# The first block's down-projection by seven products, and the differences of w_down made earlier, one operation at a time

## The chip, the cores and the metric

The kernel runs on one core of a Trainium2 chip. A core has a matrix engine (TensorE, PE in the profile, with its weight loads as PEld), a vector engine (VectorE, DVE), a scalar engine (ScalarE, ACT), a general engine (GpSimd, POOL) and an engine that here only issues transfers (SyncE, SP). Each takes its own instructions in order; transfers (DMA) run on 16 engines of their own and are issued from the queues of SP, ACT and POOL. The metric is the time of one execution on the device, in microseconds (us).

## The reference: what is computed

One layer of an encoder is computed for 2048 prompt rows and for 8 x 16 = 128 sample rows: 17 tiles of 128 rows, of width 1024. The first half is attention and a recurrent memory, whose results are joined and multiplied by `w_out`. The second half, which the change touches, is a feed-forward network with a convolution of width 3 over the rows:

```python
    mix = jnp.concatenate([att, mlstm_out], axis=-1) @ w_out
    x = x + rms_norm(mix, norm_g[1])
    ffn, new_buf = conv_ffn(rms_norm(x, norm_g[2]), conv_buf, w_up, w_conv, b_conv, w_down)
    x = x + rms_norm(ffn, norm_g[3])

def conv_ffn(h, buf, w_up, w_conv, b_conv, w_down):
    u = h @ w_up                                   # 1024 -> 2 * 2816
    ext = jnp.concatenate([buf.astype(u.dtype), u], axis=1)
    y = b_conv
    for j in range(CONV_W):
        y = y + ext[:, j:j + S] * w_conv[j]
    gate, up = jnp.split(y, 2, axis=-1)
    out = (jax.nn.gelu(gate, approximate=True) * up) @ w_down   # 2816 -> 1024
```

All of it is float32.

## The kernel before

A float32 product is made of three matrix instructions on rounded parts: each operand is split into a high part (ScalarE's copy with rounding) and a low part (VectorE's subtraction), and `mm3` adds high times high, high times low and low times high. `split` is that pair of operations; in the profile it has lines 1308 (ScalarE) and 1309 (VectorE), and the three matrix instructions have lines 104 to 106.

The stages follow one another. First the input projection runs with attention and memory between its products. Then `project` goes through the 17 tiles of w_out: per tile it multiplies two halves of 512 columns (each eight triples of instructions, `wo`), normalizes them (`mx`), and meanwhile prepares the next tile: POOL computes a scale (`att_ms`, `att_rs`), VectorE applies it (`mr`), TensorE transposes (`mT_pt`), ScalarE and VectorE split the result (`mt`, lines 210 and 211). During the last part of w_out the rows of the first block of the feed-forward network are prepared as well (`h2_units`).

The feed-forward network works on three blocks of tiles: six, six and five. Each has an up stage, then a down stage.

The up stage goes through 22 groups of 128 columns of the hidden width (named by f), each with a gate and an up half. It multiplies by Strassen's scheme, seven products in place of eight, which needs sums and differences of quarters of w_up. They are made in the first block's up stage: four quarters are loaded (`wu`, by SP), VectorE makes four more (`ws`, line 1325), POOL stores them to memory (`wsd`, line 1327), and the later blocks load them. The quarters share 11 buffers (`quad`), so a load waits until a buffer is free. After the products come the convolution (POOL copies two columns from and to `halo`, lines 1494 and 1499; ScalarE and VectorE, lines 1502 to 1504), the activation and the product of the halves.

The down stage has two forms. Blocks listed in `FAST` use seven products too: during their up stage `store_a` writes the quarters of the activations and their sums (`A11`, `A12`, `A22`, `S1` to `S4`) to memory in `ad`, S1 and S4 partly by transfers that add to what is there, and makes S3 and S2 by one subtraction each (`s`, line 1597). This needs f and f + 11 together, so such a block goes through the groups in the order 0, 11, 1, 12 and so on. In the down stage seven products of 11 steps over three pairs of tiles follow (`SEQUENCE`), each with a quarter of `w_down` or one of its combinations T1 to T4; `leave` adds the results up. A block that isn't in `FAST` stores the activations whole (`gd`), and its down stage goes twice (for two halves of the columns) through 22 steps over six tiles, with `down` and `evacuate`.

Before, the second and third blocks are in `FAST`, and the first isn't. The combinations T1 to T4 are made during the first block's down stage by `folds`: for each of 11 row groups ScalarE issues the loads of four quarters into the six buffers of `spare`, VectorE makes four combinations in place (`fold`, line 1180), one after another, and POOL stores them (`wtd`, line 1185).

The order on each engine is set by the framework's scheduler, which places instructions by its own estimate of time; `keep_in_program_order` holds the instructions so marked in the order in which they were written. In the first half and in w_out, `pump` chooses between streams of work by costs that each step yields, and `h2_units` is such a stream.

## Time and profile before

| | us |
|---|---|
| median of 3 runs | 2763.57 |
| lowest and highest | 2761.47, 2770.18 |
| profiled execution | 2763.96 |
| its span, first to last instruction | 2762.2 |

The granted clock of TensorE is 0.997 over the span. In the rows of the profile, `uec`, `ua` and `ub` are the accumulators of the up stage, `dn` and `dnm` those of the down stage, `wdh` and `wdl` the split parts of a quarter of w_down, `gh` and `gl` those of the activations in the dense form, `ah` and `al` in the form by seven products. "L1309 DVE TENSOR_TENSOR wul<-wu,wuh ... x255 | 165.1, 683 | 3.7" is a group of 255 operations on line 1309 with 165.1 us in all, 683 ns each, and 3.7 us of idle time ahead of them. A row of a table of waits has the engine and line that waited, what it waited for, the sum in us, how often, and the longest.

### The profile page before, as it was taken

The page shows a single profiled execution, that of the slowest core. Times are in us where ns is not written, and L with a number is a line of the kernel's source. Part 1 is how long each engine was busy: PE and PEld are TensorE (multiplying, and loading weights), DVE is VectorE, ACT ScalarE, POOL GpSimd, SP SyncE. Part 2 cuts the span into 40 slices and gives each one's busy share as a digit, 9 for nine tenths or more (in the row PEclk, how much of TensorE's full clock was granted, in tenths as well). Part 3 has the DMA queues.
Part 4 walks back from the last instruction along what each step waited for, and adds up shares of the span by engine and source line. Part 5 has one row for each costly group of instructions (what it writes and reads, how often), then busy time and mean ns, then how long its engine had stood idle before and what let it go on. Part 6 is the DMA issues. An engine that isn't in the chain of part 4 may idle for free.

```text
span 2762.2 us, 47713 instructions
## 1 busy us (share of the span) xinstructions
PE 2692.4 (97%) x16422; PEld 2520.0 (91%) x16422; DVE 1902.5 (69%) x3593; ACT 1437.1 (52%) x2918; POOL 627.4 (23%) x1276
## 2 busy tenths in 40 slices
PE   7899999999999999999999999999999999999998
PEld 7899999998899998888999998789999878999976
DVE  5345445646546567655999988558888875998956
ACT  4355545635356566544554555435554665555554
POOL 1000010211100011222333322123443212555401
PEclk9999999999999999999999999999999999999999
DMA  5534355547564456355645559867886777788775
GB/s 180 161 117 137 106 158 166 170 146 215 155 187 132 139 169 196 120 171 177 239 166 182 166 174 337 297 230 202 242 241 189 244 238 245 217 261 247 249 264 184
DMA packets 329185, 539.72 MB, mean 195 GB/s; under 512 B 60354, under 2 KB 162974, under 8 KB 328814
## 3 DMA queue, kind: packets, MB, share of 16 engines
q1 hardware_dynamic: 248382, 393.82, 46.1%
q0 software_dynamic: 35632, 97.48, 11.3%
q10 hardware_dynamic: 44928, 45.37, 5.0%
q8 instruction: 129, 2.11, 0.3%
q14 instruction: 114, 0.93, 0.1%
HBM read 383.28 MB, written 162.68 MB: 198 GB/s over the span
## 4 chain that ended last, share of the span: by engine, by line
PE 79%; DMA 10%; DVE 5%; ACT 2%; issue 2%; POOL 1%; SPq 0%; ACTq 0%; DVEq 0%; POOLq 0%
PE uec L104 6%; PE uec L105 6%; PE uec L106 6%; PE dn L106 4%; PE dn L104 4%; PE dn L105 4%; PE ua L106 3%; PE ua L105 3%; PE ua L104 3%; PE qb L105 2%; PE qb L106 2%; PE qb L104 2%; PE pt L76 2%; PE wo L106 2%; PE wo L105 2%
## 5 line engine op out<-in xcount | busy, mean ns | idle before, releaser
L104 PE MATMUL uec<-B,wuh 128*128 128x384 f32 (+1 forms) x720 | 236.0, 328 | 2.5 <-DVE uu L1645 2.5
L105 PE MATMUL uec<-B,wuh 128*128 128x384 f32 (+1 forms) x720 | 235.1, 327 | 0.0
L106 PE MATMUL uec<-B,wul 128*128 128x384 f32 (+1 forms) x720 | 233.7, 327 | 0.0
L1308 ACT CAST wuh<-wu 128x512 fp32r<-128x512 f32 x255 | 141.7, 618 | 107.8 <-PE uec L105 98.6
L1309 DVE TENSOR_TENSOR wul<-wu,wuh 128x512 fp32r<-128x512 f32 x255 | 165.1, 683 | 3.7 <-DMA x2d<-mx 2.3
L405 DVE CUSTOM_DVE_ANT_0 tmp<-s,nb 128x640 f32<-128x640 f32 (+4 forms) x128 | 94.4, 737 | 93.9 <-PE s L395 92.1
L104 PE MATMUL vo<-wi_h,hT 128*128 128x256 f32 x544 | 155.2, 285 | 0.7 <-DVE mt L211 0.6
L106 PE MATMUL vo<-wi_h,hT 128*128 128x256 f32 x544 | 155.6, 286 | 0.0
L105 PE MATMUL vo<-wi_l,hT 128*128 128x256 f32 x544 | 154.8, 285 | 0.0
L104 PEld LDWEIGHTS uec<-B,wuh 128*128 128x128 f32 x720 | 135.1, 188 | 5.4 <-DVE uu L1645 4.1
L104 PE MATMUL qk<-hT,wi_h 128*128 128x384 f32 (+1 forms) x384 | 128.5, 335 | 7.4 <-ACT qk_st L236 6.7
L105 PEld LDWEIGHTS uec<-B,wuh 128*128 128x128 f32 x720 | 135.2, 188 | 0.2
L106 PEld LDWEIGHTS uec<-B,wul 128*128 128x128 f32 x720 | 135.1, 188 | 0.0
L418 DVE TENSOR_TENSOR ptl<-pt,pth 128x640 fp32r<-128x640 f32 (+4 forms) x128 | 93.6, 738 | 57.4 <-ACT pth L417 56.4
L406 ACT ACTIVATE tmp<-tmp,mn 128x640 f32<-128x640 f32 (+4 forms) x128 | 97.6, 763 | 66.1 <-DVE mn L405 64.7
L1309 DVE TENSOR_TENSOR wdl<-wdr,wdh 128x512 fp32r<-128x512 f32 x198 | 125.0, 685 | 7.8 <-ACT wdh L1308 7.6
L105 PE MATMUL qb<-hT,wi_h 128*128 128x384 f32 (+1 forms) x384 | 127.9, 333 | 0.0
L105 PE MATMUL qk<-hT,wi_h 128*128 128x384 f32 (+1 forms) x384 | 127.8, 333 | 0.0
L106 PE MATMUL qk<-hT,wi_l 128*128 128x384 f32 (+1 forms) x384 | 127.4, 332 | 0.0
L106 PE MATMUL qb<-hT,wi_l 128*128 128x384 f32 (+1 forms) x384 | 127.3, 331 | 0.0
L104 PE MATMUL qb<-hT,wi_h 128*128 128x384 f32 (+1 forms) x384 | 127.2, 331 | 0.0
L106 PE MATMUL dn<-wdh,al 128*128 128x512 f32 x308 | 124.1, 403 | 2.6 <-DVE al L1309 2.6
(447 smaller groups left out, 9271.1 us busy)
## 6 DMA issues: line engine op xcount, KB each, us to landing
wu<-in_w_up SPq DMA_DIRECT2D x220, 256.0 KB, 4.9
wu<-wsd SPq DMA_DIRECT2D x176, 256.0 KB, 5.0
wdr<-in_w_down SPq DMA_DIRECT2D x110, 256.0 KB, 5.3
wi_raw<-in_w_in SPq DMA_DIRECT2D x52, 512.0 KB, 4.0
wsd<-ws POOLq DMA_DIRECT2D x88, 256.0 KB, 3.8
wdr<-wtd SPq DMA_DIRECT2D x88, 256.0 KB, 5.3
gr<-gd SPq DMA_DIRECT2D x39, 384.0 KB, 6.1
kraw<-kTd SPq DMA_DIRECT2D x112, 128.0 KB, 3.3
```

The lines of the kernel that those rows point to most:

```text
L76: nc.tensor.transpose(out, in_, ident[:n, :n])
L104: nc.tensor.matmul(out, ah, bh, start=start, stop=False, skip_group_check=onto)
L105: nc.tensor.matmul(out, ah, bl, start=False, stop=False, skip_group_check=onto)
L106: nc.tensor.matmul(out, al, bh, start=False, stop=stop, skip_group_check=onto)
L405: nc.vector.tensor_tensor_reduce(o_, s_, b_, 1.0, 3e38, ALU.add, ALU.min, accum_out=mn)
L406: nc.scalar.activation(tmp[:, :n], tmp[:, :n], AF.Exp, bias=mn, scale=-1.0, accum_out=rsum[:, i % 4, hh:hh + 1])
L418: nc.vector.tensor_tensor(s.ptl[:, sl, qc], ptv, s.pth[:, sl, qc], op=ALU.subtract)
L1308: nc.scalar.copy(h, r)
L1309: nc.vector.tensor_tensor(l, r, h, op=ALU.subtract)
```

## The change

The first block is put into `FAST`, so its up stage stores by `store_a` and goes through the groups in pairs, and its down stage runs by `SEQUENCE`. Since that stage reads T1 to T4 itself, they are made earlier: `folds` is written anew as one generator over units, and `project` advances it by one step at each half accumulation, 66 steps for 11 units over the 68 half accumulations of 17 tiles. A unit loads two quarters, two steps later the other two, and then makes one combination per step; the fourth is left to the start of the next unit, with the four stores behind it. The engines stay the same: loads issued by ScalarE, combinations by VectorE, stores by POOL. The kind "U" in the code, for w_up, isn't used (`UPS` is empty).

```diff
-FAST = (1, 2)
+UPS = []
+WOUT_FOLDS = [("T", k) for k in range(NK)] + [("U", f) for f in UPS]
+FAST = (0, 1, 2)
...
+        fold, owed = folds(WOUT_FOLDS), [0.0]
         load(ss[0])
         norm(ss[0])
...
                     if k % 4 == 3:
+                        owed[0] += 6 * len(WOUT_FOLDS) / 66
+                        while owed[0] >= 1:
+                            owed[0] -= 1
+                            next(fold, None)
                         yield 2.6, 0.5
...
+        for _ in fold:
+            pass
...
+    def folds(units):
+
+        keep = tc.keep_in_program_order
+        sub, plus = ALU.subtract, ALU.add
+        ahead = None
+        for n_, (what, k) in enumerate(units):
+            src, dst = (I["w_down"], wtd) if what == "T" else (I["w_up"], wsd)
+            part = lambda d, x: d[k][:, x * 512:(x + 1) * 512]
+            if ahead:
+                ahead()
+            q = [spare_tile(f"fold{what}{k}_{x}") for x in range(2)]
+            for x in range(2):
+                keep(nc.scalar.dma_start(q[x], part(src, x)))
+            yield
+            yield
+            q += [spare_tile(f"fold{what}{k}_{x}") for x in (2, 3)]
+            for x in (2, 3):
+                keep(nc.scalar.dma_start(q[x], part(src, x)))
+            yield
+            a, b, c, d = q
+            if what == "T":
+                ops = [(a, b, a, sub), (b, c, b, sub), (c, a, c, sub), (d, d, c, plus)]
+                out = [a, b, c, d]
...
+            for o, x, y, op in ops[:3]:
+                keep(nc.vector.tensor_tensor(o, x, y, op=op))
                 yield
-        if live:
-            store(NK - 1)
+
+            def ahead(out=out, dst=dst, k=k, last=ops[3]):
+                o, x, y, op = last
+                keep(nc.vector.tensor_tensor(o, x, y, op=op))
+                for i, t in enumerate(out):
+                    keep(nc.gpsimd.dma_start(dst[k][:, i * 512:(i + 1) * 512], t))
+        ahead()
...
-    fold = folds(4, {0: ("ab",), 1: ("cd",), 3: ("combine", "store")})
...
-                    if b == 0:
-                        next(fold, None)
...
-        if b == 0:
-            for _ in fold:
-                pass
```

What that makes of the order is shown at three places. VectorE in w_out, tile 13 of 17, before: `mx13` is that tile's result, `mt14` the split of the next tile, `mr15` the scaling of the one after it, `t42` belongs to the preparation of the first block.

```order
L1026 TENSOR_TENSOR mx13_15890<-wo13_0_15892,norm_row1_13117 128x512
L211 TENSOR_TENSOR mt14_15882<-mT14_pt0_15937,mt14_15882 128x1024
L1026 TENSOR_TENSOR mx13_15890<-wo13_1_15950,norm_row1_13117 128x512
L1145 TENSOR_TENSOR t42_15982<-h2T_pt2_0_1_15975,t22_15912 128x512
L1038 SCALAR_TENSOR_TENSOR mx13_15890<-mx13_15890,n1_13_rs_15991 128x1024
L997 TENSOR_SCALAR mr15_15948<-mr15_15948,att15_rs_16000 128x512
```

The same place after; `foldT9` are the four quarters of unit 9:

```order
L1203 TENSOR_TENSOR foldT9_0_15971<-foldT9_1_15972,foldT9_0_15971 128x512
L1033 TENSOR_TENSOR mx13_16023<-wo13_0_16025,norm_row1_13102 128x512
L213 TENSOR_TENSOR mt14_16015<-mT14_pt0_16075,mt14_16015 128x1024
L1203 TENSOR_TENSOR foldT9_1_15972<-foldT9_2_16038,foldT9_1_15972 128x512
L1033 TENSOR_TENSOR mx13_16023<-wo13_1_16088,norm_row1_13102 128x512
L1203 TENSOR_TENSOR foldT9_2_16038<-foldT9_0_15971,foldT9_2_16038 128x512
L1154 TENSOR_TENSOR t42_16122<-h2T_pt2_0_1_16115,t22_16049 128x512
L1045 SCALAR_TENSOR_TENSOR mx13_16023<-mx13_16023,n1_13_rs_16131 128x1024
L999 TENSOR_SCALAR mr15_16086<-mr15_16086,att15_rs_16140 128x512
L1208 TENSOR_TENSOR foldT9_3_16039<-foldT9_3_16039,foldT9_2_16038 128x512
```

The four operations of the unit now stand singly between the steps of the tile; none of the tile's own steps has changed its place.

POOL in the first block's up stage, from one group's `uu` copy to the next's, before: `halo` copies, four stores of w_up differences (`wsd`) and one store of activations (`gd`).

```order
L1494 COPY uu0_8_17533<-halo_15158 128x2
L1663 DMA gd0_6_213<-g0_6_17288 128x768
L1494 COPY ug0_8_17543<-halo_15158 128x2
L1499 COPY halo_15158<-ug0_7_17390 128x2
L1499 COPY halo_15158<-uu0_8_17533 128x2
L1327 DMA wsd10_264<-ws10_0_17611 128x512
L1327 DMA wsd10_264<-ws10_1_17612 128x512
L1327 DMA wsd10_264<-ws10_2_17613 128x512
L1494 COPY uu0_9_17688<-halo_15158 128x2
```

After, between two such copies (`ad0` is the first block's store of quarters and sums):

```order
L1509 COPY uu0_9_19319<-halo_15218 128x2
L1343 DMA wsd10_249<-ws10_0_19395 128x512
L1591 DMA ad0_A11_207<-y0_8_0_19060 128x384
L1597 DMA ad0_S1_210<-y0_8_0_19060 128x384
L1514 COPY halo_15218<-ug0_19_19165 128x2
L1343 DMA wsd10_249<-ws10_1_19396 128x512
L1509 COPY ug0_9_19329<-halo_15218 128x2
L1614 DMA ad0_S3_212<-s3_0_8_19223 128x384
L1343 DMA wsd10_249<-ws10_2_19397 128x512
L1343 DMA wsd10_249<-ws10_3_19398 128x512
L1514 COPY halo_15218<-uu0_9_19319 128x2
L1509 COPY uu0_20_19472<-halo_15218 128x2
```

The transfers to `ad` stand between the stores of w_up differences and the copies that the next convolution needs.

VectorE in the same stage, around the product of the two halves, before (`ws12` are differences of w_up, `y0_9` the convolution of the next group):

```order
L1325 TENSOR_TENSOR ws12_0_17919<-wu12_3_17917,wu12_2_17915 128x512
L1655 TENSOR_TENSOR g0_8_17596<-y0_8_0_17591,y0_8_1_17585 128x768
L1325 TENSOR_TENSOR ws12_1_17920<-ws12_0_17919,wu12_0_17911 128x512
L1503 SCALAR_TENSOR_TENSOR y0_9_1_17740<-uu0_9_17688,wcv_16205,y0_9_1_17740 128x768
L1483 TENSOR_TENSOR ug0_9_17698<-x1_0_9_17635,uec0_9_17633 128x384
```

After, from the same product to the first of the two subtractions (`s3`):

```order
L1670 TENSOR_TENSOR y0_8_0_19060<-y0_8_0_19060,y0_8_1_19054 128x768
L1519 SCALAR_TENSOR_TENSOR y0_19_1_19207<-uu0_19_19155,wcv_16366,y0_19_1_19207 128x768
L1498 TENSOR_TENSOR ug0_19_19165<-x1_0_19_19102,uec0_19_19100 128x384
L1325 TENSOR_TENSOR wu30_20_0_3_19233<-ws20_2_19244,wu30_20_0_1_19231 128x512
L1341 TENSOR_TENSOR ws10_1_19396<-ws10_0_19395,wu10_0_19387 128x512
L1325 TENSOR_TENSOR wu30_20_0_3_19233<-ws20_0_19242,wu30_20_0_1_19231 128x512
L1612 TENSOR_TENSOR s3_0_8_19223<-y0_8_0_19060 128x384
```

The subtraction stands six rows behind the product, among the splits of the next weights.

24 lines of the change are left out of this document (3 added, 21 removed).

## The prediction

> **What bounds the kernel now.** I read the page's first part, then the whole program cut into stages, then who TensorE and VectorE waited for in the stages that the change touches. The page:
>
> ```profile
> span 2762.2 us, 47713 instructions
> PE 2692.4 (97%) x16422; PEld 2520.0 (91%) x16422; DVE 1902.5 (69%) x3593; ACT 1437.1 (52%) x2918; POOL 627.4 (23%) x1276
> ```
>
> TensorE is busy nearly throughout, so products taken out shorten the span only where nothing else takes their place. The stages, in order: w_out, first block up and down, second block up and down, third block up (each row: stretch, its length, busy time of each engine, granted clock, DMA share):
>
> ```profile
> core 0: us, PE busy (x) PEld busy (x) DVE busy (x) ACT busy (x) POOL busy (x), PEclk, DMA share, GB/s
> 1053.00:1322.00 269.00, 265.51 (x1437) 224.00 (x1437) 165.34 (x306) 132.71 (x319) 64.65 (x124) 1.00 0.52 166
> 1322.00:1639.00 317.00, 316.30 (x1807) 313.95 (x1806) 294.43 (x446) 164.58 (x264) 108.98 (x187) 1.00 0.53 180
> 1639.00:1839.30 200.30, 194.57 (x869) 157.92 (x868) 139.12 (x200) 93.97 (x159) 39.18 (x75) 1.00 0.86 289
> 1839.40:2157.60 318.20, 317.82 (x1824) 317.34 (x1822) 264.34 (x399) 162.11 (x270) 120.07 (x217) 1.00 0.76 217
> 2157.70:2330.30 172.60, 172.00 (x769) 139.00 (x770) 123.95 (x186) 108.82 (x200) 30.91 (x46) 1.00 0.76 250
> 2335.00:2615.00 280.00, 275.33 (x1841) 272.23 (x1840) 247.16 (x509) 151.58 (x264) 151.62 (x313) 0.99 0.81 241
> ```
>
> The reader is to see a model for the change inside the trace. The second block has as many tiles as the first (six) and already uses seven products: its down stage lasts 172.6 us, the first block's 200.3. Both up stages last 317 to 318 us with TensorE full, but in the first VectorE is at 294.4 of 317.0 (93%), since it also makes the differences of w_up there; in the second at 83%.
>
> **Part 1: the down stage, 22 x 6 x 2 products against 7 x 11 x 3.** In matrix instructions, three each: 792 against 693, so 99 fewer of 128x512. Their spacing, first and last of ten consecutive rows (start, duration):
>
> ```profile
> 1699.80 0.40 PE L106 MATMUL dn<-wdh,gl 128*128 128x512 f32 x1
> ...
> 1701.90 0.40 PE L106 MATMUL dn<-wdh,gl 128*128 128x512 f32 x1
> ```
>
> Nine steps in 2.10 us are 0.233 us each (the 0.40 overlap), so 99 x 0.233 = 23.1 us. The difference of the stages is larger, 200.3 - 172.6 = 27.7, because TensorE idled 200.30 - 194.57 = 5.7 us in the dense one and 0.6 in the other. What it waited for in the dense stage:
>
> ```profile
> PE dn L104 <- DVE fr L1393: 2.0, 2, 1.5
> PE h2T_pt L1106 <- ACT b L1123: 1.7, 1, 1.7
> PE dn L104 <- DVE ug L1483: 1.1, 2, 0.9
> PE h2T_pt L1106 <- DVE t L1132: 0.8, 1, 0.8
> ```
>
> The evacuation `fr` between the halves goes with the dense form; the moved differences leave this stage too, with the waits for the landing of their stores (`wtd<-fold`) that stand ahead of `gh` on ScalarE:
>
> ```profile
> ACT gh L1308 <- DMA wtd<-fold: 13.6, 3, 4.9
> ```
>
> The 33 more weight quarter-tiles split here (77 against 44) cost VectorE 33 x 0.685 and are in the second block's 123.95 us, 72% of its stage. While it runs, this stage transposes the next block's tiles, six where the model has five:
>
> ```profile
> L1106 PE MATMUL h2T_pt<-ident,x2r 128*128 128x128 f32 x48 | 7.6, 273 | 2.5 <-ACT b L1123 1.7 <-DVE t L1132 0.8
> L1106 PE MATMUL h2T_pt<-ident,x2r 128*128 128x128 f32 (+1 forms) x48 | 6.8, 261 | 0.0
> ```
>
> 7.6 against 6.8: 0.8 us are taken off the 27.7. I take -27; the ends are -28 (all of the model) and -22 (products alone, and a microsecond of new waits).
>
> **Part 2: the first block's up stage.** It loses 22 stores of `gd` and gains, per pair of column groups, nine transfers to `ad`, two subtractions (`s3`, `s2`) and waits of POOL for two accumulating transfers. Prices from the second block's up stage, of which ten of eleven pairs lie in the window:
>
> ```profile
> L1597 DVE TENSOR_TENSOR s<-s,y 128x384 f32<-128x384 f32 x10 | 5.5, 553 | 0.1
> L1597 DVE TENSOR_TENSOR s<-y 128x384 f32<-128x384 f32 x10 | 5.5, 552 | 0.0
> L1576 POOL DMA_DIRECT2D ad_A<-y x30 | 18.1, 603 | 16.8 <-DVE y L1655 16.6 <-DVE y L1503 0.2
> L1600 POOL DMA_DIRECT2D ad_S<-s x10 | 9.0, 903 | 19.2 <-DMA ad_S<-y 15.5 <-DVE f L1429 3.5
> ```
>
> VectorE: 22 x 0.553 = 12.2 us, which brings it to 294.4 + 12.2 = 306.6 of 317 (96.7%). POOL: 99 transfers between 0.603 and 0.903, say 0.7, are 69; 22 of `gd` go, at most 0.603 by the nearest plain row, 13; so 109 + 56 = 165, 52%, plus some 15 of waiting on landings. Behind a waiting POOL stand its stores of w_up differences, which free the buffers into which SP loads the next w_up, and the two-column halo copies that ScalarE's convolution step needs. Whether that shows depends on VectorE's free time (its waits in this stage, then two of SP's queue):
>
> ```profile
> DVE ug L1483 <- PE uec L106: 7.5, 4, 2.3
> DVE uu L1645 <- PE uec L106: 5.0, 8, 1.2
> DVE ws L1325 <- DMA wu<-in_w_up: 4.6, 8, 1.4
> DVE y L1503 <- issue: 1.7, 6, 0.3
> DVE uu L1483 <- PE uec L106: 1.4, 3, 0.5
> ...
> SPq L1320 <- DVE wul L1309: 149.8, 41, 12.6
> ...
> SPq L1320 <- DMA wsd<-ws: 17.5, 4, 6.2
> ```
>
> Of the 317.0 - 294.4 = 22.6 us that VectorE idles, 13.9 (7.5, 5.0, 1.4) are spent waiting for TensorE: that is slack, and 12.2 fits into it with little over. The 4.6 behind loads is not slack. Nearest for a crowded stage is the third block's: POOL 54%, VectorE 88%, TensorE idle 280.0 - 275.3 = 4.7 us. I take +4, between 0 (all in the slack) and +12.2 (every new subtraction exposed). A gain is excluded: TensorE idles only 0.7 us there now.
>
> **Part 3: the w_out stage.** The 44 operations on w_down move here from the down stage, one step per half accumulation, with 44 loads issued by ScalarE and 44 stores by POOL. Price, from where they stand now:
>
> ```profile
> L1180 DVE TENSOR_TENSOR fold<-fold,fold 128x512 f32<-128x512 f32 x44 | 30.1, 685 | 1.9 <-DMA fold<-in_w_down 1.5
> L1185 POOL DMA_DIRECT2D wtd<-fold x44 | 24.2, 551 | 103.3 <-DVE fold L1180 100.5 <-issue 2.4
> ```
>
> VectorE goes from 165.3 to 195.4 of 269 (73%), POOL from 64.7 to 88.9, DMA has half its time free. What hides them: VectorE's wait for ScalarE's copy ahead of each `mt`. One tile, in rows of three engines:
>
> ```profile
> 1260.03 1.28 DVE L1038 SCALAR_TENSOR_TENSOR mx<-mx,n_rs 128x1024 f32<-128x1024 f32 x1 [0.80 <-POOL n_rs L93]
> 1262.03 0.48 DVE L997 TENSOR_SCALAR mr<-mr,att_rs 128x512 f32<-128x512 f32 x1 [0.72 <-POOL att_rs L93]
> ...
> 1268.20 1.23 DVE L211 TENSOR_TENSOR mt<-mT_pt,mt 128x1024 fp32r<-128x1024 f32 x1 [5.09 <-ACT mt L210]
> ...
> 1260.08 1.29 POOL L87 TENSOR_SCALAR att_ms<-assq 128x1 f32<-128x1 f32 x1
> ...
> 1263.97 0.19 POOL L87 TENSOR_SCALAR wssq<-wssq 128x1 f32<-128x1 f32 x1 [1.98 <-ACT mx L1028]
> ...
> 1266.03 1.04 PE L76 MATMUL mT_pt<-ident,mr 128*128 128x128 f32 x8
> ...
> 1269.48 0.50 PE L106 MATMUL wo<-wo,mt 128*128 128x512 f32 x1 [0.33 <-DVE mt L211]
> ```
>
> VectorE idles 5.09 us before `mt`, enough for seven of the moved operations. But `mt` itself is on the edge: TensorE waited 0.33 us for it. A moved operation that starts just ahead of it adds up to 0.685 per tile, 17 x 0.685 = 11.6 if it always does. ScalarE's load of a unit's third and fourth quarter must wait for the store of the previous unit's first two, and its copies queue behind. I take +3, about a quarter of 11.6; the ends are +43.7 (all 44 operations exposed, 30.1, and ScalarE's 13.6 of waiting for their stores as well) and -3.5, the idle time of TensorE in this stage (269.0 - 265.5), which the new order could close.
>
> Here POOL's `att_ms` took 1.29 us just while VectorE's 1.28 us `mx` ran, and the same operation on another tile's `wssq` 0.19. The Trainium skill, SBUF — State Buffer, section "SBUF: two separate sides", says that VectorE and GpSimd share one port pair under an exclusive lock, which an operation of VectorE with two SBUF inputs takes against a GpSimd operation that reads SBUF. The moved operations have two SBUF inputs, so by that rule `att_ms` and `att_rs` may each be held 0.685 longer, 1.37 per tile; the rows agree with the rule. Without it the sum stays as written; with it the chain to `mr` grows by 17 x 1.37 = 23.3, but `mr` ended at 1262.5, 3.5 us before TensorE took it at 1266.0, so the path still gets nothing.
>
> **The sum.** The profiled execution took 2763.96 us, 1.8 more than its span and 0.4 above the median of the three runs (2763.57). -27 + 4 + 3 = -20: 2744. From the sixth column group of the second block's up stage on, every engine's order is the same in both kernels, and so it is up to the beginning of w_out: 0 for the rest.
>
> **Rivals.**
> First, the first block's up stage becomes bound by VectorE and POOL: the 12.2 us are exposed in full, because the 4.6 behind loads grow when POOL's stores free the buffers later. For it: 96.7%, and SP's queue, which already waits for buffers most of the time (149.8 and 17.5 us). Against: the load stays below one, and TensorE idles 0.7 us at 93%. 2763.96 - 27 + 12.2 + 3 = 2752.
> Second, the down stage gives only its products: the waits come back as waits for the first splits of `ah` and the weights. 2763.96 - 22 + 4 + 3 = 2749. Against: the model's 0.6 us of idling.
> Third, on the other side: in w_out the moved units stand on the chain `mx`, `mr`, `mT`, `mt`, on VectorE by their operations and on ScalarE by the loads that wait for stores, and delay each tile's products. Fully exposed, 43.7: 2763.96 - 27 + 4 + 43.7 = 2785. It decides from 23 us on (27 - 4), about half of that. For it: `mt` without slack; against: 5 us of idling before it and 73% load.
> That the seven products would not be made is out: TensorE's order has the 99 fewer.
>
> **Chances.** Forecast 2744 (2737 to 2748) 0.68; down stage gives only its products 0.09; up stage bound 0.14; w_out exposed 0.09. A run of this kernel tells 0.3% from no change, 8.3 us, so faster means under 2755.3: all of the first two, 0.09 of the third, 0.01 of the fourth, 0.87; no change 0.05 of the third and 0.02 of the fourth, 0.07; slower 0.06. Range: 2734, where w_out gains its 3.5 and the up stage costs nothing (-28 - 3.5 = -31.5 would be 2732), to 2757, beyond the first rival; some 0.05 lie below, 0.1 above.
>
> **What would show it.** The stage from the first to the last `dn` of the first block near 173 us, with VectorE near 124; the up stage within 5 us of 317, with VectorE near 307 and its waits for `uec` mostly gone; w_out within 4 us of 269, TensorE's waits for `mt` a little larger. The prediction is wrong if the up stage lasts over 329, if TensorE's waits in w_out for `mt` or `mT_pt` pass 15, or if the down stage stays above 180.

## The result, and the profile after

The forecast was 2744 us; the change made no gain. The changed kernel took 2772.41 us (median of 22 runs, 2760.67 to 2778.48) beside 2765.83 for the kernel before: the ratio is 1.0019, 95% interval 1.0012 to 1.0027. Two later sessions gave 1.0027 (1.0015 to 1.0040) and 1.0027 (1.0009 to 1.0046).

The first profiled execution of the changed kernel, 2760.67 us, is the shortest of its 22 runs. A third profile, labelled again2 below, took 2774.01 us, near the median, and is shown here as the profile after. Its first lines:

```profile
span 2772.3 us, 47858 instructions
...
PE 2684.6 (97%) x16323; PEld 2509.7 (91%) x16323; DVE 1923.8 (69%) x3643; ACT 1457.4 (53%) x2961; POOL 697.3 (25%) x1353
```

The 99 matrix instructions are gone (16422 before), and the span is longer all the same. The same execution by stages, in the form used in the prediction (start and end, length, busy time and instructions of PE, PEld, DVE, ACT, POOL, granted clock, DMA share, GB/s). The rows are cut after the same number of TensorE's instructions as the rows of before (99 fewer from the first down stage on), so they hold nearly the same work: w_out, first block's up stage, its down stage, second block's up stage.

```profile
1051.60:1345.90 294.30, 274.46 (x1437) 229.56 (x1437) 188.51 (x347) 133.57 (x322) 89.38 (x167) 0.96 0.69 228
1345.90:1666.80 320.90, 316.72 (x1807) 313.62 (x1806) 306.85 (x474) 165.21 (x260) 169.54 (x259) 1.00 0.68 209
1666.80:1844.20 177.40, 174.11 (x770) 140.74 (x769) 126.77 (x186) 112.97 (x204) 26.51 (x46) 0.99 0.78 249
1844.20:2162.40 318.20, 317.74 (x1823) 317.37 (x1822) 261.64 (x394) 161.96 (x269) 118.38 (x207) 1.00 0.75 213
```

Cut in the same way, the first block's up and down stage before are:

```profile
1322.00:1638.90 316.90, 316.20 (x1807) 313.85 (x1806) 294.43 (x446) 164.48 (x264) 108.98 (x187) 1.00 0.53 180
1638.90:1839.40 200.50, 194.77 (x869) 158.12 (x868) 139.22 (x200) 94.17 (x159) 39.28 (x75) 1.00 0.86 289
```

Beside the rows of before, the down stage went from 200.5 to 177.4 us (-23.1), the up stage from 316.9 to 320.9 (+4.0), and w_out from 269.0 to 294.3 (+25.3) for the same 1437 matrix instructions. The gain was given back ahead of the place where it is made. The other two profiles of the changed kernel have 291.2 and 290.7 us in w_out, 320.1 and 320.5 in the up stage, 176.5 and 175.6 in the down stage.

Of the 25.3 us in w_out, 16.3 are idle time of TensorE (294.3 - 274.46 = 19.8 against 3.5), and 9.0 are longer instructions (274.46 against 265.51 busy); the granted clock of the stage is 0.96. By the trace's record of the clock, TensorE ran at half rate for 23.9 us of this stage, in three stretches that begin at 1085, 1225 and 1324 us; before the change there is none in w_out, and the two short profiles have 13.65 us. What TensorE waited for there (line that waited, releaser, sum in us, times, longest):

```profile
PE wo L108 <- DVE mt L213: 6.5, 1, 6.5
PE ot L432 <- ACT pth L419: 4.0, 1, 4.0
PE h2T_pt L1115 <- DVE x2r L1107: 3.0, 2, 2.8
```

Before, these three were 1.2, 0.3 and 0.4. The three sums rest on three long waits, near the starts of the three slow stretches, rather than on a delay in every tile. The time from the first `wo` product of a tile to that of the next shows it (for tile 17, to the last product of w_out); the table has the difference to the kernel before in us, from the start times in the traces (each kernel is described below). Each row is one profiled execution; the two other profiles of the changed kernel have sums of 21.5 and 20.9:

| kernel | tiles 1-2 | 3-8 | 9-10 | 11-16 | 17 | sum |
|---|---|---|---|---|---|---|
| changed (again2) | 7.0 | 0.7 | 6.9 | 1.4 | 8.7 | 24.6 |
| no combinations (none) | 0.2 | 0 | -0.5 | 0 | -0.2 | -0.3 |
| no operations (nodve) | 4.9 | 0 | 2.1 | 0.4 | 6.5 | 13.9 |
| no transfers (notraffic) | 7.0 | 0.2 | -0.3 | 0.8 | 0.2 | 7.9 |
| no stores (nostore) | 7.3 | 0.6 | 2.4 | 1.4 | 5.6 | 17.3 |
| 1.5 steps from tile 1 (fast12) | 2.1 | 8.7 | 1.3 | 1.3 | -0.5 | 12.9 |
| 1.5 steps from tile 3 (mid2) | 0.1 | 3.9 | 3.8 | 0.5 | -0.4 | 7.9 |
| 2 steps from tile 6 (mid5) | 0.4 | 5.0 | 6.8 | 3.5 | -0.5 | 15.2 |

**The last tile.** Before, in rows of SP, VectorE and TensorE: SP issues the first four quarters of w_up, VectorE's first difference of them (`ws`) waits for the last, the three other differences follow, and behind them stands `mt`, the low part of the last tile, which the third of its products needs:

```profile
1297.67 1.64 SPq L1320 DMA_DIRECT2D wu<-in_w_up  x3
...
1304.38 0.69 DVE L1325 TENSOR_TENSOR ws<-wu,wu 128x512 f32<-128x512 f32 x1 [2.90 <-DMA wu<-in_w_up]
...
1306.91 1.22 DVE L211 TENSOR_TENSOR mt<-mT_pt,mt 128x1024 fp32r<-128x1024 f32 x1
...
1308.18 0.50 PE L106 MATMUL wo<-wo,mt 128*128 128x512 f32 x1 [0.50 <-DVE mt L211]
```

After, rows of the same engines:

```profile
1313.60 1.14 SPq L1336 DMA_DIRECT2D wu<-in_w_up  x1
...
1324.90 0.69 DVE L1341 TENSOR_TENSOR ws<-wu,wu 128x512 f32<-128x512 f32 x1 [8.72 <-DMA wu<-in_w_up]
...
1327.44 1.22 DVE L213 TENSOR_TENSOR mt<-mT_pt,mt 128x1024 fp32r<-128x1024 f32 x1
...
1328.71 0.80 PE L108 MATMUL wo<-wo,mt 128*128 128x512 f32 x1 [6.55 <-DVE mt L213]
1329.31 0.63 PE L106 MATMUL wo<-wo,mt 128*128 128x512 f32 x1
```

Before, the last quarter is the third of the three issued in one row; after, it has a row of its own. From the end of the issue to the operation that waits for the last quarter it was 5.1 us before (1304.38 - 1299.31) and 10.2 after (1324.90 - 1314.74), while the DMA engines were 0.92 busy from 1310 to 1325. The order, `ws` ahead of `mt`, is that of the kernel before: there the wait of 2.90 used up the slack and 0.50 showed. After, 8.72 us of waiting showed as 6.55.

**The first two tiles.** Here the scheduler placed the instructions otherwise. On ScalarE, `pth` (a split for the attention, which TensorE's `ot` needs) stood ahead of `mvo` before:

```profile
1081.52 1.29 ACT L417 CAST pth<-pt 128x640 fp32r<-128x640 f32 x2 [0.47 <-PE ot L430]
...
1083.70 0.41 ACT L660 ACTIVATE mvo<-mvo 128x256 f32<-128x256 f32 x1
```

Now it stands behind `mvo`, which waits for a load of its own; rows of ScalarE and TensorE in the profile after:

```profile
1085.31 0.42 ACT L662 ACTIVATE mvo<-mvo 128x256 f32<-128x256 f32 x1 [2.46 <-DMA mvo<-vobd]
...
1086.21 0.67 ACT L419 CAST pth<-pt 128x640 fp32r<-128x640 f32 x1
...
1087.53 0.58 PE L432 MATMUL ot<-pth,vhl 128*128 128x256 f32 x1 [3.97 <-ACT pth L419]
```

That wait of 3.97 us is the largest part of the 7.0 us that the table has for the first two tiles; the rest isn't traced to single instructions.

**The ninth tile.** The rows of the residual that the preparation of the first block reads back arrive late: over the stage ScalarE waited 8.1 us in four times for `x2r<-x2d` (line 1103), where the kernel before has 1.0 us in two. The longest of the four stands here; POOL's scale and VectorE's `x2r` then came late, and TensorE waited for them; rows of ScalarE and TensorE:

```profile
1221.13 1.06 ACT L1103 ACTIVATE B<-x2r 128x1024 fp32r<-128x1024 f32 x1 [3.95 <-DMA x2r<-x2d]
...
1224.66 0.63 PE L1115 MATMUL h2T_pt<-ident,x2r 128*128 128x128 f32 x4 [2.81 <-DVE x2r L1107]
```

### The profile page after: what moved, and what is told of

Read it like the earlier page. It is cut to its first block, busy times and chain, and to the rows that moved or that the text cites. A ratio compares the mean times of both kernels' runs of the same rounds, so it can differ in the third digit from the quotient of the medians.

```text
span 2759.0 us, 47858 instructions
## 1 busy us (share of the span) xinstructions
PE 2676.8 (97%) x16323; PEld 2506.6 (91%) x16323; DVE 1923.1 (70%) x3643; ACT 1458.3 (53%) x2961; POOL 695.8 (25%) x1353
## 3 DMA queue, kind: packets, MB, share of 16 engines
q0 software_dynamic: 41968, 108.30, 13.3%
## 4 chain that ended last, share of the span: by engine, by line
PE 42%; DVE 4%; DMA 4%; issue 2%; ACT 1%; POOL 1%; DVEq 0%; SPq 0%; POOLq 0%; ACTq 0%
PE uec L106 5%; PE uec L107 5%; PE uec L108 5%; PE dn L108 3%; PE dn L106 3%; PE dn L107 3%; PE ua L108 3%; PE ua L106 2%; PE ua L107 2%; PE dnm L108 1%; PE dnm L107 1%; PE dnm L106 1%; PE ub L108 1%; PE ub L107 1%; PE ub L106 1%
## 5 line engine op out<-in xcount | busy, mean ns | idle before, releaser
L108 PE MATMUL dn<-wdh,al 128*128 128x512 f32 x462 | 185.3, 401 | 4.7 <-DVE al L1325 4.5
L1325 DVE TENSOR_TENSOR al<-ar,ah 128x768 fp32r<-128x768 f32 (+2 forms) x141 | 108.6, 780 | 116.0 <-ACT ah L1324 114.5
L106 PE MATMUL dn<-wdh,ah 128*128 128x512 f32 x462 | 183.0, 396 | 4.6 <-ACT ah L1324 2.9
L107 PE MATMUL dn<-wdl,ah 128*128 128x512 f32 x462 | 182.1, 394 | 0.0
L1324 ACT CAST ah<-ar 128x768 fp32r<-128x768 f32 (+2 forms) x141 | 96.2, 692 | 149.9 <-PE dnm L107 110.8
L1325 DVE TENSOR_TENSOR wdl<-wdr,wdh 128x512 fp32r<-128x512 f32 x231 | 145.4, 685 | 8.0 <-ACT wdh L1324 5.9
L1324 ACT CAST wdh<-wdr 128x512 fp32r<-128x512 f32 x231 | 127.4, 620 | 11.4 <-PE uec L107 7.3
L106 PE MATMUL qk<-hT,wi_h 128*128 128x384 f32 (+1 forms) x384 | 129.6, 337 | 3.6 <-ACT qk_st L238 2.8
```

Of the source, the lines that this page charges most:

```text
L106: nc.tensor.matmul(out, ah, bh, start=start, stop=False, skip_group_check=onto)
L107: nc.tensor.matmul(out, ah, bl, start=False, stop=False, skip_group_check=onto)
L108: nc.tensor.matmul(out, al, bh, start=False, stop=stop, skip_group_check=onto)
L1324: nc.scalar.copy(h, r)
L1325: nc.vector.tensor_tensor(l, r, h, op=ALU.subtract)
```

## The experiments

Four theories stood for the loss in w_out: the transfers of the combinations make other loads late (traffic); VectorE's 44 operations push `mt` back (operations); ScalarE waits for the stores and its copies queue behind (ScalarE); and the loss hangs on the place, on what else goes on beside it (places). All ratios are to the kernel before in the same session, with 95% intervals.

**again** is the changed kernel unaltered.

> The changed kernel unaltered, for a second profile of it, since its first profiled execution (2760.67 us) is the shortest of its 22 runs and its median is 2772.41. If the stretch of w_out is what varies (its loads meet its stores differently from run to run), this profile shows a w_out stage of 288 to 300 us and the other stages within 1 us of the first profile. If it is something else, such as a lower granted clock, every stage is longer by 0.3 to 0.5%, and w_out stays at 288.

2772.11 us, ratio 1.0027 (1.0015 to 1.0040); the profiled execution 2762.59. w_out lasts 290.7 us and the first block's stages are within 1 us of the first profile. But the profiled execution was again a short one, so it can't tell what makes the others longer: its granted clock is 0.994, as in the first profile, and the mean of the ten runs is 0.992 (0.996 for the kernel before in the same session). It is 5.3 us shorter than the kernel before already in the stretch ahead of w_out, where TensorE has the same order.

**none** leaves out the combinations:

```diff
-        fold, owed = folds(WOUT_FOLDS), [0.0]
+        fold, owed = iter([]), [0.0]
...
-            src = I["w_down"][k] if blk < 4 else wtd[k]
+            src = I["w_down"][k]
```

> No combinations of w_down at all: neither their 44 loads, 44 operations nor 44 stores; the seven products of the first block and of the second read the unfolded quarters of w_down from memory instead (the combinations are left out). All theories: the down stages stay at 176 and 172 us. If the moved combinations are the whole cost of w_out, that stage goes back to 269 us (within 3) and the time is 19 to 23 us under the changed kernel's, about 2750. If something else of the change made w_out longer, it stays above 275. If the first block's up stage was made longer by the tail of the combinations, it falls from 323 to 319; by its own added work, it stays at 322 to 324.

2751.47 us, ratio 0.9952 (0.9936 to 0.9968). w_out, up and down stage:

```profile
1052.80:1321.40 268.60, 265.49 (x1437) 223.83 (x1436) 165.10 (x306) 132.69 (x319) 64.04 (x124) 1.00 0.51 167
1321.40:1644.60 323.20, 317.78 (x1807) 313.59 (x1806) 305.54 (x471) 166.28 (x264) 168.50 (x259) 1.00 0.67 206
1644.60:1822.90 178.30, 174.32 (x770) 140.77 (x769) 126.60 (x186) 112.93 (x204) 24.80 (x46) 0.99 0.78 248
```

w_out is back at 269, so the moved combinations are its whole loss, and by time they cost 20.6 us (2772.11 - 2751.47). The up stage stays at 323.2: its growth, 6.3 us, comes with the seven products and not from the tail of the combinations.

**nodve** keeps loads and stores and leaves out VectorE's 44 operations:

```diff
-                keep(nc.vector.tensor_tensor(o, x, y, op=op))
                 yield
...
-                o, x, y, op = last
-                keep(nc.vector.tensor_tensor(o, x, y, op=op))
```

> All 44 loads and 44 stores of the combinations kept at their places, VectorE's 44 operations left out (the tiles are stored as they were loaded, so the combinations are not computed). Theory traffic (the loads and stores crowd the DMA queues, the first loads of w_up land late and VectorE's difference of w_up that waits for them stands ahead of mt): w_out stays at 283 to 290 us and the time within 6 us of the changed kernel's. Theory operations (VectorE's 44 operations themselves push mt back): w_out falls to 269 to 273 us, the time by 15 to 20 us. Theory ScalarE (its loads wait for the stores and its copies queue behind them): w_out stays above 280, with ScalarE waiting for stores as before.

2761.66 us, ratio 0.9998 (0.9986 to 1.0009). **notraffic** keeps the operations and leaves out 40 loads and 40 stores; the first unit's four loads stay, at the first tile:

```diff
-            q = [spare_tile(f"fold{what}{k}_{x}") for x in range(2)]
-            for x in range(2):
+            if n_ == 0:
+                q = [spare_tile(f"fold{what}{k}_{x}") for x in range(2)]
+            for x in range(2 if n_ == 0 else 0):
...
-                for i, t in enumerate(out):
+                for i, t in enumerate(out if k == NK - 1 else ()):
...
```

> VectorE's 44 operations kept at their places, but on the same four tiles all the time: only the first unit's four loads and the last unit's four stores are left, the other 40 loads and 40 stores are left out (the down stages read the unfolded quarters). Theory traffic: w_out falls to 269 to 274 us, the time by 14 to 20 us. Theory operations: w_out stays at 283 to 290 us. Theory ScalarE (waiting for stores): falls to 272 or less as well, since nothing is waited for; the run without VectorE's operations then tells it from traffic by ScalarE's waits. A sum of both causes would put this run and the one without VectorE's operations each in between, near 278.

2751.46 us, ratio 0.9957 (0.9943 to 0.9972), as without any combinations. w_out by stages lasts 283.6 us in the first and 276.9 in the second. What VectorE and TensorE wait for in it, without the operations:

```profile
DVE ws L1338 <- DMA wu<-in_w_up: 9.3, 1, 9.3
...
PE wo L108 <- DVE mt L213: 5.3, 2, 4.9
```

And without the transfers:

```profile
DVE ws L1343 <- DMA wu<-in_w_up: 2.9, 1, 2.9
PE ot L432 <- ACT pth L419: 3.5, 1, 3.5
```

Without the operations the wait at the last tile stays (9.3 us), without the transfers it is that of before (2.9): the transfers make it. The loss at the first two tiles stays in both. What they share is the order on ScalarE, `mvo` ahead of `pth`: without the transfers ScalarE waited 2.04 us at `mvo` and TensorE 3.55 for `pth`, without the operations TensorE waited 3.3. Where `pth` kept its place (before, `none`, and `mid2` below), that wait is 0.3. They also share the first unit's four loads, issued by ScalarE in the first tile, and no run separates these from the order. At tiles 9 and 10 the loss goes with the transfers: 2.1 us without the operations, none without the transfers.

By stages, the operations alone cost 8 us and the transfers alone 15, 25 together; by time, 0, 10 and 21. The profile sees 8 us for the operations that the timed runs, with an interval of about 4 us either way, don't show. So neither theory holds by itself: without the operations the stage is within theory traffic's 283 to 290, but the time falls by 10 us and not by at most 6; without the transfers the stage lies between the two forecasts. By time the transfers alone cost half, and the other half comes only where the operations stand beside them. In the table that half is spread over the first two tiles, tiles 9 and 10 and the last; how the operations add to it wasn't traced. Theory ScalarE is out as the main cause: its waits for `foldT` are 7.2 us in one event in again2, behind which TensorE waited 0.49 and 0.34 us.

**nostore** keeps loads and operations, with stores of the last unit alone:

```diff
-                for i, t in enumerate(out):
+                for i, t in enumerate(out if k == NK - 1 else ()):
...
```

> The changed kernel's 44 loads and 44 operations at their places, but only the last unit's four stores (40 stores are left out, and the down stages read the unfolded quarters). It halves the added traffic, 11.5 of 23 MB. If the crowding by bytes is what delays the first loads of w_up, the last tile is 2 to 5 us longer than without combinations (8 with all of it) and the time is near 2757. If the stores alone are to blame (they wait in POOL's queue and free the six buffers), the last tile is within 1 us and the time is that of the run without traffic, 2751 to 2754. If the loads alone, it stays above 2765.

2765.83 us, ratio 0.9998 (0.9983 to 1.0014). VectorE's wait for the first quarters of w_up lies between the others, and so does the last tile (+5.6 us):

```profile
DVE ws L1341 <- DMA wu<-in_w_up: 5.7, 1, 5.7
...
PE wo L108 <- DVE mt L213: 3.5, 1, 3.5
```

Half the added bytes give about half of the added wait: 2.9 and 5.7 us with nearly none and half of the transfers, and 8.7, 9.5 and 9.7 in the three profiles with all. The time is higher than the 2757 expected for bytes alone. By the ratios to the kernel before, the loads cost 11 us (0.9998 against 0.9957) and the stores 8 (1.0027 against 0.9998), each with an interval of several us; which weigh more isn't shown.

**hold** pins VectorE's order, so that `ws` stands behind the last `mt`:

```diff
-            nc.vector.tensor_tensor(lv, ptv, hv, op=ALU.subtract)
+            sub_ = nc.vector.tensor_tensor(lv, ptv, hv, op=ALU.subtract)
+            if name[:2] == "mT":
+                tc.keep_in_program_order(sub_)
...
-                nc.vector.tensor_tensor(o, x, y, op=op)
+                op_ = nc.vector.tensor_tensor(o, x, y, op=op)
+                if f == 0:
+                    tc.keep_in_program_order(op_)
```

> The changed kernel with two kinds of VectorE operation pinned: the subtractions mt of w_out keep their written order, and the first group's differences of w_up (ws) stand behind the last of them, so that an operation that waits for a load of w_up can no longer stand ahead of mt of the last tile. Traffic with this wait as its way into the path: TensorE's 7.8 us of waiting for mt falls below 1.5, w_out from 287 to 276 to 280 us, and the time by 6 to 11 us (the two with the slow matrix instructions behind the wait); the first block's up stage grows by 0 to 3, since its first difference starts later. If that wait is only one of several that follow each other (the next late load stops another operation), w_out stays above 283 us and the time within 4 us.

2771.62 us, ratio 1.0014 (1.0000 to 1.0027). The wait for `mt` is gone and the last tile 0.4 us shorter than before, but the beginning of the up stage now waits. w_out and up stage (here the cut lies 10 us behind the first product of the up stage, so the first row holds the first of these waits):

```profile
1058.30:1342.00 283.70, 270.25 (x1437) 225.27 (x1436) 190.73 (x348) 137.60 (x324) 87.93 (x168) 0.99 0.73 238
1342.00:1671.50 329.50, 322.37 (x1806) 318.57 (x1806) 305.23 (x473) 162.06 (x258) 163.46 (x257) 0.98 0.66 203
```

Rows of VectorE, ScalarE and TensorE at the beginning of the up stage:

```profile
1336.11 0.69 DVE L1343 TENSOR_TENSOR ws<-wu,wu 128x512 f32<-128x512 f32 x1
...
1336.90 1.88 ACT L1326 CAST wuh<-ws 128x512 fp32r<-128x512 f32 x3
...
1338.23 0.44 PE L106 MATMUL ub<-B,wuh 128*128 128x384 f32 x1 [3.88 <-ACT wuh L1326]
```

What w_out gained, the up stage lost (8.6 us against again2). But the run doesn't show that late loads stop the next user: the first `ws` waited for no load any more. Held behind the last `mt`, it ran after the last tile's normalization, so late that its split and TensorE's `ub` waited for it. A second wait of 2.52 us, at 1350.10, has a late load behind it (ScalarE waited 4.55 for `wu<-in_w_up`). So `hold` shows that this order only moves the loss.

**fast12** makes the combinations at 1.5 steps per half accumulation, so that they end ahead of the first loads of w_up:

```diff
-                        owed[0] += 6 * len(WOUT_FOLDS) / 66
+                        owed[0] += 1.5
```

> The combinations stay in w_out but run at 1.5 steps per half accumulation in place of one, so that they are done by the twelfth tile, ahead of the first loads of w_up. If the crowding at the end of w_out (its loads and stores against the first loads of w_up, attention's and the copies of the residual) is what costs, w_out falls to 272 to 278 us and the time by 8 to 14 us. If the combinations cost the same wherever they stand in w_out, because the 23 MB of transfers or VectorE's operations push mt back tile by tile, w_out stays at 284 to 292 us and the time within 4 us. A denser stream could also make it worse: ScalarE's waits for stores would then pass 15 us.

2762.45 us, ratio 0.9977 (0.9966 to 0.9987), with 281.9 us in w_out. The last tile is whole again (-0.5 us) and `ws` waits 2.4 us; but tiles 3 to 8, beside the end of the attention (its last `ot` stands in tile 8), lose 8.7.

**early** makes them from the second half of the input projection on; the last operation stands at 1094 us.

```diff
-        fold, owed = folds(WOUT_FOLDS), [0.0]
+        fold, owed = iter([]), [0.0]
...
+    fold, owed = folds(WOUT_FOLDS), [0.0]
...
+            if half == 1 and gi >= 2:
+                owed[0] += 0.45
+                while owed[0] >= 1:
+                    owed[0] -= 1
+                    next(fold, None)
...
```

> The same combinations done in the second half of the input projection instead of w_out, one every second group piece, finished before w_out begins. The DMA share is 0.48 to 0.63 there before the change and VectorE is at 46 to 69%, TensorE full. If it is the place at the end of w_out that costs, w_out goes back to 269 us, the part ahead of it grows by 0 to 5 us from 1051, and the time is near the run with no combinations, 2752 to 2757. If 44 combinations cost some 20 us wherever they are put beside full work, the part ahead of w_out grows by 10 us or more and the time stays above 2763.

2782.57 us, ratio 1.0050 (1.0032 to 1.0068). The first 7286 instructions of TensorE and the next 1437, as before; but the order is another here, and the first product of w_out already stands at 1066.7 (1053.9 before), with 79 fewer instructions ahead of it:

```profile
0.00:1081.60 1081.60, 1021.34 (x7286) 989.95 (x7287) 595.46 (x1434) 543.84 (x1292) 116.91 (x327) 0.99 0.58 174
1081.60:1351.80 270.20, 264.92 (x1437) 223.29 (x1436) 164.75 (x315) 130.24 (x317) 63.05 (x127) 1.00 0.52 168
```

The second stretch is nearly that of before (270.2 against 269.0), with the last tile whole (-0.4 us), and the first is 28.6 us longer (1053.0 before). A DMA share of 0.5 to 0.6 and a VectorE under 70% didn't mean room. TensorE's longest sums of waiting there are for ScalarE's `tmp` (7.6 us) and `skh` (6.8); which of the moved instructions holds them up wasn't separated.

**dense** is the move alone, with the first block's down stage as before:

```diff
-FAST = (0, 1, 2)
+FAST = (1, 2)
```

> The move alone: the combinations of w_down in w_out as in the changed kernel, and the first block's down stage in its dense form (22 by 6 by 2 triples), as before. Moving costs what the changed kernel shows: w_out 284 to 289 us. The first block's up stage 315 to 318 (it has none of the new transfers and subtractions), its down stage 196 to 204 counted from dn to uec (the waits for their landing are gone from it). Time 2776 to 2786: the kernel before plus 18 for w_out, less up to 5. If the up stage here is also near 323, its growth comes from the tail of the combinations and not from the seven products.

2792.64 us, ratio 1.0083 (1.0059 to 1.0107), above the 2776 to 2786 expected. w_out, up and down stage:

```profile
1055.30:1346.70 291.40, 273.10 (x1437) 228.73 (x1436) 189.05 (x347) 133.70 (x322) 88.78 (x167) 0.97 0.71 231
1346.70:1665.80 319.10, 316.80 (x1807) 313.74 (x1806) 295.74 (x449) 163.67 (x261) 111.95 (x188) 1.00 0.54 181
1665.80:1865.00 199.20, 194.83 (x869) 158.14 (x868) 113.07 (x157) 94.14 (x159) 14.96 (x32) 1.00 0.56 179
```

The move costs 22.4 us in w_out and frees the down stage of 1.3. So where they stood, the combinations (30.1 us of VectorE) cost next to nothing.

**mid2** starts at the third tile at 1.5 steps, its last operation falling in the fourteenth; **mid5** starts at the sixth with two steps. The edit of mid2 (mid5 has `2 if n_ >= 5`):

```diff
-                        owed[0] += 6 * len(WOUT_FOLDS) / 66
+                        owed[0] += 1.5 if n_ >= 2 else 0
```

> The combinations start at the third tile of w_out, at 1.5 steps per half accumulation, and are done by about the thirteenth: neither beside the first two tiles, where the changed kernel, the one without the operations and the one without the traffic all lose 5 to 7 us, nor beside the last, where the first loads of w_up land. If those two places are the cost, with some 3 us at the ninth tile, the w_out stage is 3 to 6 us above the kernel with no combinations, and the time 2755 to 2759. If each combination costs by its own traffic wherever it stands, the loss moves to the middle tiles, and the time stays at the 2762 of the run at 1.5 steps from the first tile.

> The combinations start at the sixth tile, two steps per half accumulation, and are done by the fourteenth: beside the tiles where the attention has nearly ended. By the theory of places: like the run from the third tile or 1 to 3 us better at tiles 2 to 7, unless the end of its stores meets the first loads of w_up again, which would show as a wait of VectorE for such a load above 5 us and a last tile 4 to 8 us longer; the time 2754 to 2762. By the theory of cost by traffic: a denser stream makes tiles 6 to 13 each 1 to 2 us longer, and the time is 2760 to 2766.

mid2 took 2749.55 us, ratio 0.9937 (0.9917 to 0.9956), and is the fastest kernel of the study that does all the work: faster than the kernel before and the changed one, and below the 2755 to 2759 expected. Its w_out and down stage:

```profile
1049.30:1326.20 276.90, 268.21 (x1438) 224.56 (x1437) 189.46 (x350) 133.21 (x318) 87.58 (x166) 0.99 0.76 245
...
1647.30:1821.90 174.60, 171.94 (x770) 139.96 (x769) 127.47 (x186) 112.07 (x204) 28.04 (x48) 1.00 0.79 254
```

VectorE's wait for the first quarters of w_up is 2.5 us, as before the change. The same 44 loads, operations and stores, at a higher DMA share (0.76 against 0.69), cost 8 us of w_out instead of 25. ScalarE's waits for these loads and stores are longer here, 13.7 us, one more sign against the theory ScalarE. mid5 took 2760.20 us, ratio 0.9990 (0.9973 to 1.0006): its last tile is whole, but the denser stream costs 15 us between tiles 7 and 16 (its profiled execution, 2767.89 us, is one of the longer ones). Both theories of the expectation have a share: leaving the two places takes most of the loss away, and the stream with two steps costs at other tiles.

**again2** is the changed kernel a third time.

> The changed kernel unaltered once more, for a third profile. Both of its profiled executions so far (2760.67 and 2762.59 us) are the shortest of their runs, whose medians are 2772. If that is chance of the stretch ahead of w_out, which varies by some 5 us either way with the same order of instructions, this profile lies between 2760 and 2778 and its part from w_out on is within 2 us of the others. If profiled executions of this kernel differ from timed ones, it is below 2765 again.

2773.50 us in eight runs, ratio 1.0027; this profile is a typical one. It is 13.3 us longer than the first: 2.3 ahead of w_out, 3.1 in it, 1.7 in the first block's two stages and 6.2 behind the second block's up stage. Its clock is 0.991, against 0.994 in the two short ones.

**before2** and **mid2b** repeat the kernel before and mid2.

> The kernel before, unaltered, for a second profile. In its first profile the stretch from the second block's down stage to the end lasted 604.6 us; in ten profiles of other kernels it lasted 603.7 to 610.8, though the work there is the same. If that stretch only varies from run to run, it lies between 603 and 611 here too and may pass 606. If the first block's new form makes it longer (the order of the stores and loads ahead of it differs), it stays within 1 us of 604.6.

> The run with the combinations from the third to the thirteenth tile once more, unaltered, for a narrower interval and a second profile. Its ratio to the kernel before was 0.9937 (0.9917 to 0.9956): again 0.992 to 0.996, with a w_out stage of 274 to 278 us. If the first was a lucky draw, 0.996 or more.

before2 took 2765.79 us, ratio 1.0001 (0.9991 to 1.0011). From the second block's down stage on it needs 608.5 us, where the first profile had 604.6; w_out (268.9) and the up stage (317.7) are the same. That stretch varies from run to run, and nothing in it is the change's. mid2b took 2752.30 us, ratio 0.9947 (0.9933 to 0.9961), with 274.1 us in w_out: the gain of mid2 repeats, 13 to 17 us.

## Why the prediction was wrong

The step that failed is Part 3: the term of +3 for the w_out stage measured +22 to +25, within its own ends (up to 43.7), but far from the value taken. Three things in its working were wrong.

First, it priced the moved operations by one tile with 5 us of idle time ahead of `mt` and asked how many operations fit in, and it gave the transfers no price of their own. Without their transfers the operations cost nothing that the timed runs show, the transfers without operations 10 us, and both together 21. "DMA has half its time free" was read from 0.52, the mean of the stage; at its end, where the first loads of w_up are issued, the share was higher already before the change (0.70, then 0.82):

```profile
1295.00:1305.00 10.00, 10.00 (x50) 8.17 (x49) 4.36 (x6) 2.84 (x8) 2.84 (x5) 1.00 0.70 210
1305.00:1322.00 17.00, 16.50 (x76) 13.55 (x75) 11.00 (x17) 6.45 (x13) 5.26 (x11) 1.00 0.82 272
```

Second, Part 3 asked what is queued behind the moved instructions, and not which waits of others grow: VectorE's `ws` waited 2.90 us for those loads before, directly ahead of `mt`, and TensorE was already 0.50 late; the prediction doesn't have this row. Third, it took the order of the rest as unchanged. At the first two tiles the scheduler turned ScalarE's order round, and 5 to 7 us were lost there without the moved operations, and also with the first unit's loads as the only ones; 3.3 to 4.0 of them are TensorE's wait for `pth`.

Part 1 was nearly right: -27 taken; -23.1 in the profile shown, -24.0 and -24.9 in the two others. The busy time of TensorE fell by 20.7 to 22.3 us where 23.1 were worked out (194.8 to 174.1, 172.5 and 172.6), VectorE is at 126.8 where near 124 was forecast, and TensorE idles 3.3 us where the model has 0.6. So about 3 us of the 5.7 didn't go, and they are waits for the first splits, as the second rival had it:

```profile
PE dn L108 <- DVE al L1325: 2.0, 2, 1.9
PE dn L106 <- ACT wdh L1324: 1.1, 2, 0.6
```

Part 2 was right in size: +4 taken, +3.2 to +4.0 in the changed kernel and +6.3 where w_out isn't disturbed. VectorE's 306.6 came out at 306.85, POOL's 165 at 169.5, and the waits for `uec` are mostly gone (3.6 us of 13.9). VectorE's waits for the loads of w_up grew from 4.6 to 9.9, as the first rival had it, but its 12.2 us of exposed work did not come.

Taken without the combinations, Parts 1 and 2 gained 12 to 13 us of time where 23 were forecast. Their stages give 16: -22.2, which is the end that the second rival had, and +6.3; the other 3 to 4 lie within what a profile varies, as before2 shows. So the sum would have been some 10 us too low without the combinations as well.

The third rival, with a chance of 0.09, named the outcome: w_out exposed by about half of 43.7, from 23 us on. It had the place, and `mt` without slack, but as its mechanism the units' own operations and ScalarE's loads; at the last tile the runs show another stream's loads, made late by the units' transfers. The gauge was wrong as well: the prediction wanted over 15 us of TensorE's waits for `mt` or `mT_pt`, and there were 9.6 in a stage 25 us longer (6.5 for VectorE's part of `mt`, 3.1 for ScalarE's). None of the three signs that were to show the prediction wrong came; what failed is that w_out should stay within 4 us of 269.

The rule of the Trainium skill on the shared port (SBUF — State Buffer, section "SBUF: two separate sides") was expected to hold `att_ms` and `att_rs` longer without any effect on the path. The two operations of POOL, before and after (count, sum, mean ns):

```profile
L87 POOL TENSOR_SCALAR att_ms<-assq 128x1 f32<-128x1 f32 x16 | 17.3, 1081 | 4.1 <-ACT mt L995 3.0
...
L93 POOL TENSOR_TENSOR att_rs<-att_ms,nhalf 128x1 f32<-128x1 f32 x16 | 9.5, 594 | 1.3
```

```profile
L89 POOL TENSOR_SCALAR att_ms<-assq 128x1 f32<-128x1 f32 x16 | 15.9, 996 | 2.5 <-ACT mt L997 1.2
...
L95 POOL TENSOR_TENSOR att_rs<-att_ms,nhalf 128x1 f32<-128x1 f32 x16 | 9.8, 611 | 1.3
```

The means show no lengthening to speak of. `att_ms` meets none of the added operations in this trace; `att_rs` meets one in 2 of its 16 times, at 1103 and 1261 us, and lasted 0.89 and 0.87 us there, against 0.55 in 13 of the other 14 (0.89 in one, beside another operation of VectorE, `wo`). That fits the rule, but the two seldom meet.

What stays open: w_out, the up and the down stage of the three profiles of the changed kernel add up to 0 to +6 us against before, the timed runs to +5 to +9. The +6 are those of the typical profile, which has 23.9 us at half clock in w_out where the short ones have 13.65; whether the clock also makes the rest wasn't separated. Open as well are the share of the first unit's loads at the first two tiles and how the operations add to what the transfers cost.

## What to carry to other kernels

Before work with transfers is moved, look for the waits for DMA that other streams already have at the new place, and for what stands behind them on the same engine: a wait of 2.9 us with no slack behind it grew to 8.7 and held TensorE for 6.55. Read the DMA share in the stretch that the loads need, not in the mean of the stage, and let the moved stream end before the next stage's first loads begin: starting two tiles later and running at 1.5 times the rate turned +0.2 to 0.3% into -0.5 to -0.6%. And look at the order of every engine around the new place, since a scheduler can turn work that the change doesn't touch. A run without the operations and one without the transfers don't add up to the whole: here half of the cost needed both.

## What the runs showed of the hardware

A load took longer with more in flight: from the end of its issue to its use, the same quarter of 256 KB took 5.1 us with the DMA engines at about 0.7 busy, and 10.2 at 0.92. Without the moved transfers its user waited as briefly as before (2.9 us).

A wait of TensorE costs more than itself. After the pause of 6.55 us the products of 128x512 came every 0.427 us in place of 0.233, until 1334.43: 13 steps took 5.72 us where 13 x 0.233 are 3.03, a part of the 9 us of longer busy time. The granted clock in that stretch (third number from the end of each row):

```profile
1327.00:1330.00 3.00, 1.29 (x3) 1.10 (x4) 2.86 (x4) 0.11 (x1) 1.24 (x3) 0.50 0.97 300
1330.00:1335.00 5.00, 5.00 (x14) 3.84 (x14) 2.58 (x3) 2.76 (x6) 0.81 (x2) 0.55 0.96 337
1335.00:1340.00 5.00, 5.00 (x23) 4.04 (x22) 1.29 (x2) 0.69 (x2) 1.40 (x4) 1.00 0.18 50
```

The Trainium skill (TensorE: Matmul & The Clock Gate, "Part 1: The HAM clock gate") has the clock at half after an idle window of about 3.4 us, and back after a busy one. The trace agrees on the half rate; the slow stretch lasted 5.7 us here after the pause. In the trace's record of the clock the three stretches at half rate in w_out last 6.83, 6.83 and 10.24 us, and 3.41, 3.41 and 6.83 in each of the two other profiles: multiples of 3.41. After the pause of 0.50 us before the change, the next product came 0.34 us later and the ones after it at 0.23 to 0.24.
